# A hybrid decoder layer on one core: the triangular inverse from blocks of 16 and two levels of products, where blocks of 32 stood

## The chip, the cores and the metric

The kernel runs on one core of one Trainium2 chip. The metric is the device time of one execution in microseconds (us). The engines are TensorE (PE, with its weight loads as PEld), VectorE (DVE), ScalarE (ACT), GpSimd (POOL) and the queue engine SyncE (SP). Each takes its own instructions strictly in the order in which they were written, and waits at an instruction whose inputs aren't there.

## The reference, cut to what matters

One layer over 2048 tokens of width 1024. A projection feeds two branches: RWKV-7 time mixing (8 heads of 64) and forgetting attention (8 heads of 64). Both are gated, joined and projected out. The RWKV branch is a recurrence over the tokens:

```python
def step(S, inp):
    r_t, w_t, k_t, v_t, kk_t, b_t = inp
    sa = jnp.einsum('bhvk,bhk->bhv', S, kk_t)
    S = (S * w_t[:, :, None, :]
         - sa[..., None] * b_t[:, :, None, :]
         + v_t[..., None] * k_t[:, :, None, :])
    y = jnp.einsum('bhvk,bhk->bhv', S, r_t)
    return S, y
...
y_a = _rwkv7_scan(r_h, decay.reshape(hs), k_h, v_h, kk, kk * a_h)
y_b = _fox_attention(q_f, k_f, v_f, log_f).astype(x.dtype)
y = jnp.concatenate([y_a, y_b], axis=-1) * g_path
out = y @ w_out
```

## The kernel before, in words

**The stages.** Tokens go through in two halves of 1024. For each half there is an RWKV stage and an attention ("fox") stage; then comes the output projection. Beside them run the layer norm, the weight loads and the input projections: each projection tile is 24 products of 128x512 (`ps<-ht,wsp`), given out three at a time.

**RWKV by chunks.** The recurrence is done in chunks of 64 tokens. A block `n` (8 in each half) is one pair of heads and 512 tokens, that is 8 chunks for each of two heads: 16 triangular systems of 64x64, I + A with A strictly lower triangular, stored as `am`. For each block `rwkv_elem` makes the decays and normalised keys (DVE, ACT, POOL), `rwkv_scores` the score matrices (products 64x128, masked by DVE with `maskmm`), `rwkv_solve` the inverses of the triangular systems into `qt`, and `rwkv_batch` the outputs and the state, two chunks at a time, with the state updates one after the other. `rwkv_post` normalises the outputs. The blocks go in pairs: `elems` starts block n once block n-2 is done, so the solve of an even block runs beside `rwkv_elem` of the next one, and the solve of an odd block beside the batches of the even one.

**The solve before** (lines 1266 to 1337). The 64x64 systems are cut in blocks of 32. Four ACT copies put all 32 diagonal blocks (four on the partitions, eight along the free axis) in order, a DVE transpose replicates them, and then 31 pairs of tensor_tensors on DVE eliminate one column after the other (lines 1298 to 1304), each step needing the one before. Four transposes write the inverses of the diagonal blocks into `qt`, two more prepare `nt`, and two groups of sixteen 32x32 products on PE, each followed by two ACT copies, make the lower left block.

**What sets the order.** A planner written in Python (`Driver`) runs all streams as generators against a model of the engines: `cost` (lines 167 to 193) says how long an instruction takes, and of the streams that can go on the one with the earliest time, then the lowest priority number, writes its next instructions. Projections have priority 5, the solve 0. Which projection products stand between two products of the solve is thus fixed when the kernel is built. The planner's price of an ACT copy is `(94 if sb else 51) + 0.834 * n` ns (line 181), of a DVE tensor_tensor `69 + 1.04 * n` (line 188); no engine's work lengthens another's in it. All calls pass through one helper, so that nearly every row of the profile names line 134; the rows are told apart by tiles: `rw_s` is the arena of an RWKV stage, `ht,wsp` a projection, `wsp<-wst,wsp` the split of a weight on POOL, `fx_s`, `fx_p` and `fx_v` attention, `ps` PSUM.

Of the kernel before, what the change touches and what calls it, by code (L numbers as in the profile page):

```python
# [288 lines left out]
def hymba_kernel(ctx: ExitStack, tc, x, c, emb_ln_g, emb_ln_b, w_ada, b_ada, w_in, rwkv_mix, w0,  # L289
                 w_up, a0, a_up, k_k, k_a, r_k, gn_g, gn_b, fox_bf, w_out, ln_g, ln_b, out):  # L290
    nc = tc.nc
    drv = Driver()
# [25 lines left out]
    LA = ()  # L318
    LG = (2, 2, 4, 4)
    EF = 4  # L320
    NT = 1
    WD = 3
    XL = 5
    XN = 2
# [10 lines left out]
    pb = Banks(drv, ps, range(8))  # L335
# [11 lines left out]
    def mm(o, l, r, start=True, stop=True):  # L347
        pe.matmul(o, l, r, start=start, stop=stop, skip_group_check=True)
# [181 lines left out]
    def start_consts():  # L530
# [3 lines left out]
        yield  # L534
        ts(ident, jf, 0.0, None, OP.is_equal)
        yield
        dve.memset(nhalf, -0.5)
        pool.memset(mneg, 0.0)
        ts(mneg[:, 384:512], jf, 0.0, -1e30, OP.is_gt, OP.mult)
# [726 lines left out]
    def rwkv_solve(n, u, qt):  # L1266


        while not rw.solver:
            yield 0  # L1270
        qq, mt = rw.solver.pop()
        while not rw.nt:
            yield 0
        nt_ = rw.nt.pop()
        am = u.am.ap.rearrange("p (c a s) -> p c a s", c=2, s=64)
        nt = nt_.ap.rearrange("p (k a x) -> p k a x", k=2, x=32)
        lo = lambda ci: slice(64 * ci, 64 * ci + 32)
        hi = lambda ci: slice(64 * ci + 32, 64 * ci + 64)
        ad = qq.ap[:, 0:256].rearrange("p (s a) -> p s a", a=8)
        for ci in range(2):  # L1280
            for j in range(2):
                r0 = 64 * ci + 32 * j
                act.activation(ad[r0:r0 + 32].rearrange("p s a -> p a s"), am[r0:r0 + 32, ci, :, 32 * j:32 * j + 32],
                               AF.Copy)
        for ci in range(2):
# [3 lines left out]
        u.amuse -= 1  # L1289
        if not u.amuse:  # L1290
            u.am.free()
        M = mt.ap.rearrange("p (s r) -> p s r", r=32)
        dve.transpose(M, ad[:, :, :, None].to_broadcast([128, 32, 8, 4]))
        yield
        Q = qq.ap[:, 0:256].rearrange("p (a b) -> p a b", b=32)
        act.activation(Q, qinit, AF.Copy)
        yield
        for j in range(31, 0, -1):
            i0, k = j // 4, 8 - j // 4
            t = qq.ap[:, 256:256 + k * j].rearrange("p (a b) -> p a b", b=j)  # L1300
            tt(t, Q[:, i0:8, j:j + 1].to_broadcast([128, k, j]), M[:, j:j + 1, 0:j].to_broadcast([128, k, j]), OP.mult)
            yield
            tt(Q[:, i0:8, 0:j], Q[:, i0:8, 0:j], t, OP.subtract)
            yield
        while n >= 2 and n - 2 not in u.done:
            yield 0
        yield
        qv = qt.ap.rearrange("p (a b) -> p a b", b=128)
        for ci in range(2):
            for j in range(2):  # L1310
                r0 = 64 * ci + 32 * j
                dve.transpose(qv[r0:r0 + 32, :, r0:r0 + 32].rearrange("p a (i y) -> p i a y", y=4), Q[r0:r0 + 32])
        rw.solver.append((qq, mt))
        yield
        for ci in range(2):
            dve.transpose(nt[lo(ci), 1], qv[lo(ci), :, lo(ci)])
        yield
        b = yield from pb.get()
        for a in range(8):
            for ci in range(2):  # L1320
                mm(b.ap[hi(ci), a * 32:a * 32 + 32], nt[lo(ci), 0, a, :], nt[lo(ci), 1, a, :])
        yield
        for ci in range(2):
            act.activation(fl(nt[hi(ci), 1]), b.ap[hi(ci), 0:256], AF.Copy)
        b.free()
        yield
        b = yield from pb.get()
        for a in range(8):
            for ci in range(2):
                mm(b.ap[lo(ci), a * 32:a * 32 + 32], nt[hi(ci), 1, a, :], qv[hi(ci), a, hi(ci)])  # L1330
        yield
        for ci in range(2):
            act.activation(qv[lo(ci), :, hi(ci)], b.ap[lo(ci), 0:256].rearrange("p (a x) -> p a x", x=32), AF.Copy,
                           scale=-1.0)
        b.free()
        rw.nt.append(nt_)
        yield

    def rwkv_batch(p, n, c0, bufs, u, qt, yb, dl, st):
# [127 lines left out]
    def rwkv_stream(half):  # L1467

        phase_open(f"rw{half}", F32)
        sl = phase["slots"]  # L1470
        rw.solver = [(sl.now(1), sl.now(2))]
        rw.nt = [sl.now(1) for _ in range(NT)]
        rw.z = deque()
        rw.split = [0]
        rw.qt = [sl.now(2) for _ in range(2)]
# [560 lines left out]
```

## Time and profile before

| | |
|---|---|
| median of 3 runs | 1923.14 us (1916.16 to 1923.27) |
| the profiled execution | 1914.13 us, span 1912.4 us |
| busy in the span: PE | 1786.4 us (93%) |
| DVE | 1474.0 us (77%) |
| ACT | 781.2 us (41%) |
| POOL | 777.3 us (41%) |
| mean granted clock of PE | 0.973 of full speed |

The span runs from the first to the last instruction; the execution's time adds what lies around it. Busy time counts an instruction from start to end, also where it is held up while running. PE's products are pipelined, so that the mean of one is longer than its share of the time. The two RWKV stages lie at about 100 to 620 and 860 to 1350 us.

### The profile page before, as it was taken

Reading aid. Unit: us, or ns where it says so; the run is one execution under the profiler, and the core shown is the slowest. Engines: PE = TensorE matmul, PEld = TensorE weight load, DVE = VectorE, ACT = ScalarE, POOL = GpSimd, SP = SyncE. Lnnn points to the kernel's source line nnn. Section 1 sums busy time; section 2 is a strip of 40 time slices with the busy share of each in tenths; the row PEclk is TensorE's granted clock in tenths of the full one; section 3 lists DMA queues with packets and bytes.
Section 4 is the critical chain, followed back from the end, with each engine's and each line's share of the span. In section 5 each row is a group of like instructions: output and inputs, shape, how many; then the busy total and the mean of one; then the engine's idle time right before and its main releaser. Section 6 shows DMA issues by size and latency. Waiting matters only on the chain.

```text
span 1912.4 us, 30878 instructions
## 1 busy us (share of the span) xinstructions
PE 1786.4 (93%) x11049; PEld 1278.3 (67%) x11049; DVE 1474.0 (77%) x3606; ACT 781.2 (41%) x1507; POOL 777.3 (41%) x773
## 2 busy tenths in 40 slices
PE   8989989989899999999998999989999999999997
PEld 6667667767677755676676776667755564547876
DVE  5887897778874688568778887777367787877998
ACT  3464444533543266454453443533224444451000
POOL 1322341332423176633233331333216647675653
PEclk9999999989999999999999998989989998999999
DMA  9231110122113764332111121112365234213442
GB/s 282 66 120 63 51 54 23 39 66 62 44 51 94 238 197 127 99 108 71 45 44 43 47 65 34 52 47 89 122 209 165 93 114 136 79 61 107 141 138 105
DMA packets 172114, 181.31 MB, mean 95 GB/s; under 512 B 12181, under 2 KB 116198, under 8 KB 171961
## 3 DMA queue, kind: packets, MB, share of 16 engines
q1 hardware_dynamic: 171960, 179.33, 30.4%
q8 instruction: 88, 1.44, 0.3%
q14 instruction: 66, 0.53, 0.1%
HBM read 132.10 MB, written 47.13 MB: 94 GB/s over the span
## 4 chain that ended last, share of the span: by engine, by line
PE 45%; DVE 37%; ACT 6%; issue 4%; DMA 4%; POOL 3%; SPq 2%; POOLq 0%; DVEq 0%; ACTq 0%
PE ps L134 45%; DVE rw_s L134 19%; DVE arena L134 8%; ACT rw_s L134 4%; DVE small L134 4%; DVE end_s L134 3%; SPq L134 2%; DVE state L134 2%; DVE fx_p L134 1%; DMA wst<-in_w_in_dram 1%; DVE ht L134 1%; POOL wsp L134 1%; ACT arena L134 1%; POOL small L134 1%; DMA arena<-vscr 1%
## 5 line engine op out<-in xcount | busy, mean ns | idle before, releaser
L134 PE MATMUL ps<-ht,wsp 128*128 128x512 f32 x3840 | 981.3, 403 | 4.2 <-POOL wsp L134 3.5
L134 PEld LDWEIGHTS ps<-ht,wsp 128*128 128x128 f32 x3840 | 707.5, 191 | 161.0 <-issue 10.0
L134 DVE TENSOR_TENSOR rw_s<-rw_s 128x60 f32<-128x60 f32 (+24 forms) x1056 | 335.6, 321 | 51.2 <-ACT rw_s L134 24.0
L134 POOL TENSOR_TENSOR wsp<-wst,wsp 128x1024 fp32r<-128x1024 f32 x79 | 195.2, 2471 | 312.5 <-ACT wsp L134 267.8
L134 ACT ACTIVATE rw_s<-ps 64x256 f32<-64x256 f32 (+2 forms) x448 | 181.7, 418 | 264.4 <-PE ps L134 134.0
L134 PE MATMUL ps<-fx_s 67*128 67x512 f32 (+5 forms) x960 | 257.5, 390 | 4.4 <-ACT mrow L134 2.3
L134 PE MATMUL ps<-rw_s 32*32 32x32 f32 (+3 forms) x2816 | 208.2, 253 | 54.6 <-DVE rw_s L134 48.0
L134 PEld LDWEIGHTS ps<-fx_s 67*128 67x128 f32 (+1 forms) x960 | 164.2, 192 | 129.8 <-issue 70.3
L134 PEld LDWEIGHTS ps<-rw_s 32*32 32x32 f32 (+3 forms) x2816 | 179.4, 161 | 95.5 <-issue 55.9
L134 ACT ACTIVATE fx_p<-ps 128x512 f32<-128x512 f32 (+3 forms) x336 | 160.6, 521 | 182.7 <-PE ps L134 165.1
L134 POOL TENSOR_TENSOR fx_p<-fx_p 128x512 f32<-128x512 f32 (+2 forms) x160 | 188.9, 1186 | 109.1 <-PE ps L134 104.4
L134 POOL TENSOR_TENSOR small<-small,nhalf 128x8 f32<-128x8 f32 (+1 forms) x48 | 70.9, 1480 | 258.1 <-DVE small L134 174.8
L134 PE MATMUL ps<-fx_p,fx_v 128*64 128x512 f32 (+3 forms) x640 | 159.6, 559 | 1.6 <-POOL fx_p L134 1.6
L134 DVE TENSOR_TENSOR fx_p<-fx_p 128x512 f32<-128x512 f32 (+1 forms) x128 | 111.5, 871 | 64.1 <-POOL fx_p L134 62.2
L134 DVE TENSOR_REDUCE small<-ps 128x1 f32<-128x512 f32 (+1 forms) x208 | 133.8, 684 | 32.9 <-PE ps L134 32.1
L134 ACT ACTIVATE arena<-ps 128x512 f32<-128x512 f32 (+3 forms) x130 | 75.0, 579 | 174.1 <-PE ps L134 169.8
L134 ACT ACTIVATE wsp<-wst 128x1024 fp32r<-128x1024 f32 x80 | 84.2, 1053 | 143.0 <-PE ps L134 69.6
L134 POOL TENSOR_TENSOR rw_s<-rw_s,arena 128x512 f32<-128x512 f32 x64 | 82.5, 1294 | 136.9 <-ACT arena L134 89.6
L134 DVE TENSOR_TENSOR arena<-ps,arena 128x512 fp32r<-128x512 f32 (+4 forms) x108 | 73.2, 678 | 43.7 <-ACT arena L134 40.7
L134 DVE STREAM_TRANSPOSE rw_s<-rw_s 32x256 f32<-32x256 f32 (+1 forms) x112 | 61.6, 550 | 55.3 <-ACT rw_s L134 52.8
L134 ACT ACTIVATE rw_s<-rw_s 32x256 f32<-32x256 f32 (+1 forms) x144 | 83.4, 601 | 19.2 <-DVE rw_s L134 17.7
L134 DVE TENSOR_SCALAR state<-ps,dl 64x64 f32<-64x64 f32 x256 | 72.3, 282 | 19.3 <-PE ps L134 13.0
(147 smaller groups left out, 1885.2 us busy)
## 6 DMA issues: line engine op xcount, KB each, us to landing
wst<-in_w_in_dram SPq DMA_DIRECT2D x66, 512.0 KB
fx_s<-kscr SPq DMA_DIRECT2D x144, 128.0 KB
fx_s<-qscr SPq DMA_DIRECT2D x96, 128.0 KB
ada_t<-in_w_ada_dram SPq DMA_DIRECT2D x16, 512.0 KB
rw_l<-lowscr SPq DMA_DIRECT2D x32, 256.0 KB
kscr<-arena SPq DMA_DIRECT2D x32, 256.0 KB
qscr<-arena SPq DMA_DIRECT2D x32, 256.0 KB
arena<-in_x_dram SPq DMA_DIRECT2D x16, 512.0 KB
```

Source lines behind the costliest of these rows:

```text
L134: return fn(*args, **kw)
```

## The change

The diagonal blocks that are solved step by step are of 16, not 32. DVE does 15 pairs of tensor_tensors on both 16-blocks of each 32-block at once (two blocks in one access pattern). Two transposes then give the 16-block inverses in both orientations. A first group of 32 products, 16 wide and on the four diagonal corners of the array, with one scalar_tensor_tensor on DVE (which uses the new constant `u32`), and a second group of 48 products make the inverses of the 32-blocks; four ACT copies write these to `qt` and two keep what the last level needs in `x`. Two more groups of 16 products with two ACT copies each make the lower left 32-block, as before, with A read from `am` in place. The slot of `nt` goes, one slot `xu` comes. `u32` is made by three small operations at the start.

```diff
-        for ci in range(2):
-            with drv.side():
-                act.activation(nt[lo(ci), 0], am[lo(ci), ci, :, 32:64], AF.Copy)
...
-        for j in range(31, 0, -1):
-            i0, k = j // 4, 8 - j // 4
-            t = qq.ap[:, 256:256 + k * j].rearrange("p (a b) -> p a b", b=j)
-            tt(t, Q[:, i0:8, j:j + 1].to_broadcast([128, k, j]), M[:, j:j + 1, 0:j].to_broadcast([128, k, j]), OP.mult)
+        for j in range(15, 0, -1):
+            k = 4 - j // 4
+            o = (4 - k) * 32
+            t = qq.ap[:, 256:256 + 2 * k * j].rearrange("p (b i c) -> p b i c", b=2, c=j)
+            tt(t, blocks(qq.ap, 144, o + j, [32, k], [0, j]), blocks(mt.ap, 528, j * 32, [0, k], [1, j]), OP.mult)
             yield
-            tt(Q[:, i0:8, 0:j], Q[:, i0:8, 0:j], t, OP.subtract)
+            q = blocks(qq.ap, 144, o, [32, k], [1, j])
+            tt(q, q, t, OP.subtract)
             yield
...
-                dve.transpose(qv[r0:r0 + 32, :, r0:r0 + 32].rearrange("p a (i y) -> p i a y", y=4), Q[r0:r0 + 32])
...
-            dve.transpose(nt[lo(ci), 1], qv[lo(ci), :, lo(ci)])
...
-                mm(b.ap[hi(ci), a * 32:a * 32 + 32], nt[lo(ci), 0, a, :], nt[lo(ci), 1, a, :])
...
+        dve.transpose(dt.rearrange("p a (i y) -> p i a y", y=4), Q)
+        yield
+        dve.transpose(d, dt)
+        yield
+        b = yield from pb.get()
+        for a in range(8):
+            for r, ci, c in quads:
+                mm(b.ap[r, a * 16:a * 16 + 16], am[r, ci, a, c], d[r, a, 0:16])
+        yield
+        dve.scalar_tensor_tensor(tu[:, :, 0:16], b.ap[:, 0:128].rearrange("p (a x) -> p a x", x=16), u32[:, 32:33],
+                                 u32[:, None, 0:16].to_broadcast([128, 8, 16]), op0=OP.mult, op1=OP.add)
+        b.free()
...
+        b = yield from pb.get()
+        for a in range(8):
+            for r, ci, c in quads[0:2]:
+                mm(b.ap[r, 256 + a * 32:288 + a * 32], dt[r, a, :], tu[r, a, :])
+        for a in range(8):
+            for r, ci, c in quads[2:4] + quads[0:2]:
+                mm(b.ap[r, a * 32:a * 32 + 32], tu[r, a, :], dt[r, a, :])
+        yield
+        qv = qt.ap.rearrange("p (a b) -> p a b", b=128)
+        for r, ci, c in quads[0:2]:
+            act.activation(fl(x[r]), b.ap[r, 256:512], AF.Copy)
+        with drv.side():
+            for r, ci, c in quads[2:4] + quads[0:2]:
+                act.activation(qv[r, :, r], v8(b.ap[r, 0:256]), AF.Copy)
+            b.free()
+        yield
+        b = yield from pb.get()
+        for a in range(8):
+            for ci in range(2):
+                mm(b.ap[hi(ci), a * 32:a * 32 + 32], am[lo(ci), ci, a, 32:64], x[lo(ci), a, :])
```

**What stands where now.** The planner writes a new order from this. First PE, in the first half, from the last row-wise broadcast of block 3's `rwkv_elem` (`ident,rw_s`) to its second scores (`rw_s 128x128 x8`); before:

```order
L134 MATMUL ps<-ident,rw_s 128x128 x4
L134 MATMUL ps<-ht,wsp 128x512 x27
L134 MATMUL ps<-rw_s 128x128 x8
L134 MATMUL ps<-ht,wsp 128x512 x18
L134 MATMUL ps<-rw_s 128x128 x8
```

and now, at the same place:

```order
L134 MATMUL ps<-ident,rw_s 128x128 x4
L134 MATMUL ps<-ht,wsp 128x512 x24
L134 MATMUL ps<-rw_s 32x16 x32
L134 MATMUL ps<-ht,wsp 128x512 x3
L134 MATMUL ps<-rw_s 32x32 x48
L134 MATMUL ps<-ht,wsp 128x512 x3
L134 MATMUL ps<-rw_s 128x128 x8
L134 MATMUL ps<-rw_l,bones 128x512 x2
L134 MATMUL ps<-rw_s 32x32 x16
L134 MATMUL ps<-ht,wsp 128x512 x3
L134 MATMUL ps<-rw_s 128x128 x8
```

Block 2's solve, which stood behind block 3's scores before, now has its first two groups ahead of them.

Second PE, at the solve of block 3, which runs beside the batches of block 2 (`state,rw_s` and `rw_s,state` are one state step); before:

```order
L134 MATMUL ps<-rw_s,bones 32x128 x4
L134 MATMUL ps<-ht,wsp 128x512 x3
L134 MATMUL ps<-rw_s 32x32 x16
L134 MATMUL ps<-ident,rw_s 128x128
L134 MATMUL ps<-ht,wsp 128x512 x6
L134 MATMUL ps<-rw_s 32x32 x16
L134 MATMUL ps<-ht,wsp 128x512 x6
```

and now:

```order
L134 MATMUL ps<-rw_s 128x128 x4
L134 MATMUL ps<-rw_s 32x16 x32
L134 MATMUL ps<-state,rw_s 64x64 x2
L134 MATMUL ps<-rw_s,state 64x64 x2
L134 MATMUL ps<-ht,wsp 128x512 x3
L134 MATMUL ps<-rw_s 32x32 x48
L134 MATMUL ps<-state,rw_s 64x64 x2
L134 MATMUL ps<-rw_s,state 64x64 x2
L134 MATMUL ps<-ht,wsp 128x512 x3
L134 MATMUL ps<-rw_s 32x32 x16
```

The odd block's solve now lies among the state steps of the block before it, where it stood after them.

Third DVE, at the end of block 2's solve, with the key normalisation of block 3 (`rw_s<-arena,params,ps`); now:

```order
L134 SCALAR_TENSOR_TENSOR rw_s<-arena,params,ps 128x512
L134 TENSOR_TENSOR rw_s<-rw_s 128x2x4
L134 TENSOR_TENSOR rw_s<-rw_s 128x512 x2
L134 STREAM_TRANSPOSE rw_s<-rw_s 128x8x8x4
L134 SCALAR_TENSOR_TENSOR arena<-ps,params,arena 128x511
L134 SCALAR_TENSOR_TENSOR arena<-car,params,arena 128x1
L134 COPY car<-ps 128x1
L134 TENSOR_TENSOR rw_s<-rw_s 128x4x2x64
L134 STREAM_TRANSPOSE rw_s<-rw_s 128x256
L134 TENSOR_TENSOR rw_s<-rw_s 128x4x128
L134 TENSOR_TENSOR rw_s<-rw_s,arena 128x512
L134 SCALAR_TENSOR_TENSOR rw_s<-ps,u_122 128x8x16
```

Before, solve steps stood between these operations and after them; now the last step is the second row. Over the whole order, 1212 and 1218 projection products stood between the first product of an RWKV stage and the first of the attention stage that follows it, in the first and the second half; now 1020 and 1026. The others stand in the attention stages.

## Rows read from the trace of the kernel before

**Rows 1.** The page's head: span; busy time, share, instructions of each engine.

```profile
span 1912.4 us, 30878 instructions
...
PE 1786.4 (93%) x11049; PEld 1278.3 (67%) x11049; DVE 1474.0 (77%) x3606; ACT 781.2 (41%) x1507; POOL 777.3 (41%) x773
```

**Rows 2.** Busy times by stretch; columns in the first row.

```profile
core 0: us, PE busy (x) PEld busy (x) DVE busy (x) ACT busy (x) POOL busy (x), PEclk, DMA share, GB/s
100.00:600.00 500.00, 457.57 (x3372) 350.63 (x3372) 400.28 (x1151) 226.17 (x440) 162.41 (x164) 0.96 0.19 59
...
660.00:860.00 200.00, 197.50 (x1076) 127.27 (x1074) 145.50 (x296) 111.55 (x223) 119.79 (x152) 1.00 0.46 144
870.00:1350.00 480.00, 439.79 (x3313) 336.72 (x3314) 379.24 (x1120) 212.32 (x420) 150.67 (x157) 0.96 0.18 53
...
1420.00:1745.00 325.00, 315.49 (x1441) 170.09 (x1440) 245.13 (x420) 143.01 (x293) 199.96 (x202) 0.98 0.33 104
```

**Rows 3.** Products by tile and shape: count | busy us, mean ns | idle before.

```profile
L134 PE MATMUL ps<-rw_s 128*128 128x128 f32 x768 | 107.3, 287 | 6.6 <-issue 3.6 <-ACT rw_s L134 3.0
...
L134 PE MATMUL ps<-ident,rw_s 128*128 128x128 f32 x352 | 66.8, 295 | 11.3 <-POOL rw_s L134 10.4 <-DVE rw_s L134 0.5 <-ACT rw_s L134 0.4
L134 PE MATMUL ps<-state,rw_s 128*64 128x64 f32 x512 | 54.9, 246 | 16.8 <-DVE state L134 6.6 <-DVE rw_s L134 5.3 <-ACT rw_s L134 3.3
...
L134 PE MATMUL ps<-rw_s 64*128 64x128 f32 x512 | 42.6, 312 | 28.1 <-DVE rw_s L134 28.1
...
L134 PE MATMUL ps<-rw_s 32*32 32x32 f32 x1024 | 27.8, 202 | 19.9 <-DVE rw_s L134 19.9
```

**Rows 4.** The page's group of DVE's tensor_tensors on rw_s, all shapes.

```profile
L134 DVE TENSOR_TENSOR rw_s<-rw_s 128x60 f32<-128x60 f32 (+24 forms) x1056 | 335.6, 321 | 51.2 <-ACT rw_s L134 24.0
```

**Rows 5.** DVE's groups by shape, columns as in rows 3.

```profile
L134 DVE TENSOR_TENSOR rw_s<-rw_s 128x512 f32<-128x512 f32 x64 | 47.4, 760 | 1.5
...
L134 DVE STREAM_TRANSPOSE rw_s<-rw_s 32x256 f32<-32x256 f32 x96 | 41.7, 434 | 2.4
...
L134 DVE TENSOR_TENSOR rw_s<-ps,rw_s 64x128 f32<-64x128 f32 x128 | 36.8, 287 | 20.6 <-PE ps L134 18.8
...
L134 DVE TENSOR_TENSOR rw_s<-rw_s 128x28 f32<-128x28 f32 x64 | 12.4, 195 | 1.7
```

**Rows 6.** Timeline around block 3's scores: start us, us, engine, operation [idle before].

```profile
262.75 2.39 POOL L134 TENSOR_TENSOR wsp<-wst,wsp 128x1024 fp32r<-128x1024 f32 x1
262.76 2.45 DVE L134 TENSOR_TENSOR rw_s<-rw_s 128x60 f32<-128x60 f32 x1
...
267.14 5.02 DVE L134 TENSOR_TENSOR rw_s<-rw_s 128x72 f32<-128x72 f32 x7
...
267.27 6.40 PE L134 MATMUL ps<-ht,wsp 128*128 128x512 f32 x27
...
267.63 3.91 POOL L134 TENSOR_TENSOR rw_s<-rw_s,arena 128x512 f32<-128x512 f32 x3 [0.82 <-ACT rw_s L134]
...
272.08 0.74 DVE L134 SCALAR_TENSOR_TENSOR rw_s<-arena,params,ps 128x512 f32<-128x512 f32 x1
...
277.50 2.08 PE L134 MATMUL ps<-rw_s 64*128 64x128 f32 x16 [3.84 <-DVE rw_s L134]
```

**Rows 7.** Timeline of PE at block 0's solve.

```profile
175.00 0.70 PE L134 MATMUL ps<-rw_s 32*32 32x32 f32 x32
175.63 1.66 PE L134 MATMUL ps<-ht,wsp 128*128 128x512 f32 x6
177.22 0.69 PE L134 MATMUL ps<-rw_s 32*32 32x32 f32 x32
```

**Rows 8.** Timeline of PE at a head sum.

```profile
323.75 0.46 PE L134 MATMUL ps<-rw_s,bones 128*32 128x128 f32 x8
324.14 0.97 PE L134 MATMUL ps<-ht,wsp 128*128 128x512 f32 x3
```

**Rows 9.** ACT's copies of a solve from PSUM and within SBUF.

```profile
L134 ACT ACTIVATE rw_s<-rw_s 32x256 f32<-32x256 f32 x96 | 56.9, 592 | 12.5 <-DVE rw_s L134 11.0
...
L134 ACT ACTIVATE rw_s<-ps 32x256 f32<-32x256 f32 x64 | 24.1, 376 | 54.1 <-PE ps L134 53.3
```

**Rows 10.** Timeline of PE in a long run of projection products.

```profile
1357.91 14.56 PE L134 MATMUL ps<-ht,wsp 128*128 128x512 f32 x63
```

More of the change, by code (lines that the diff above doesn't have):

```diff
@@ L320, in hymba_kernel @@
     EF = 4
-    NT = 1
     WD = 3
@@ L359, in hymba_kernel @@
     qinit = const.tile([128, 8, 32], mybir.dt.bfloat16, name="qinit")
+    u32 = const.tile([128, 33], F32, name="u32")
     nhalf = const.tile([128, 16], F32, name="nhalf")
@@ L536, in start_consts @@
         yield
+        dve.tensor_reduce(u32[:, 0:32], ident.rearrange("p (q c) -> p c q", c=32), AX.X, OP.add)
+        yield
+        dve.tensor_reduce(u32[:, 32:33], u32[:, 0:16], AX.X, OP.add)
+        yield
+        ts(u32[:, 32:33], u32[:, 32:33], -1.0, None, OP.add)
         dve.memset(nhalf, -0.5)
@@ L1270, in rwkv_solve @@
             yield 0
[L1271 to L1274, printed above, removed]
+        qq, mt, xu = rw.solver.pop()
         am = u.am.ap.rearrange("p (c a s) -> p c a s", c=2, s=64)
-        nt = nt_.ap.rearrange("p (k a x) -> p k a x", k=2, x=32)
         lo = lambda ci: slice(64 * ci, 64 * ci + 32)
         hi = lambda ci: slice(64 * ci + 32, 64 * ci + 64)
+        quads = [(slice(64 * ci + 32 * j, 64 * ci + 32 * j + 32), ci, slice(32 * j, 32 * j + 32))
+                 for j in range(2) for ci in range(2)]
+        v8 = lambda ap: ap.rearrange("p (a x) -> p a x", a=8)
         ad = qq.ap[:, 0:256].rearrange("p (s a) -> p s a", a=8)
-        for ci in range(2):
[L1281 to L1285, printed above, removed]
-            with drv.side():
-                act.activation(nt[lo(ci), 0], am[lo(ci), ci, :, 32:64], AF.Copy)
+        for r, ci, c in quads:
+            act.activation(ad[r].rearrange("p s a -> p a s"), am[r, ci, :, c], AF.Copy)
         yield
-        u.amuse -= 1
-        if not u.amuse:
-            u.am.free()
         M = mt.ap.rearrange("p (s r) -> p s r", r=32)
@@ L1297, in rwkv_solve, with blocks @@
         yield
-        for j in range(31, 0, -1):
-            i0, k = j // 4, 8 - j // 4
-            t = qq.ap[:, 256:256 + k * j].rearrange("p (a b) -> p a b", b=j)
-            tt(t, Q[:, i0:8, j:j + 1].to_broadcast([128, k, j]), M[:, j:j + 1, 0:j].to_broadcast([128, k, j]), OP.mult)
+        def blocks(t, step, off, *dims):
+            return bass.AP(tensor=t.tensor, offset=t.offset + off, ap=[list(t.ap)[0], [step, 2], *dims])
+        for j in range(15, 0, -1):
[3 more added lines that the diff above has]
+            tt(t, blocks(qq.ap, 144, o + j, [32, k], [0, j]), blocks(mt.ap, 528, j * 32, [0, k], [1, j]), OP.mult)
             yield
-            tt(Q[:, i0:8, 0:j], Q[:, i0:8, 0:j], t, OP.subtract)
+            q = blocks(qq.ap, 144, o, [32, k], [1, j])
+            tt(q, q, t, OP.subtract)
             yield
+        dt, d, x, tu = v8(mt.ap[:, 0:256]), v8(qq.ap[:, 256:512]), v8(mt.ap[:, 256:512]), v8(xu.ap[:, 0:256])
+        dve.transpose(dt.rearrange("p a (i y) -> p i a y", y=4), Q)
[4 more added lines that the diff above has]
+        for a in range(8):
+            for r, ci, c in quads:
+                mm(b.ap[r, a * 16:a * 16 + 16], am[r, ci, a, c], d[r, a, 0:16])
[3 more added lines that the diff above has]
+        b.free()
         while n >= 2 and n - 2 not in u.done:
@@ L1320, in rwkv_solve @@
             for ci in range(2):
-                mm(b.ap[hi(ci), a * 32:a * 32 + 32], nt[lo(ci), 0, a, :], nt[lo(ci), 1, a, :])
+                mm(b.ap[hi(ci), a * 32:a * 32 + 32], am[lo(ci), ci, a, 32:64], x[lo(ci), a, :])
         yield
         for ci in range(2):
-            act.activation(fl(nt[hi(ci), 1]), b.ap[hi(ci), 0:256], AF.Copy)
+            act.activation(fl(x[hi(ci)]), b.ap[hi(ci), 0:256], AF.Copy)
         b.free()
+        u.amuse -= 1
+        if not u.amuse:
+            u.am.free()
         yield
@@ L1470, in rwkv_stream @@
         sl = phase["slots"]
-        rw.solver = [(sl.now(1), sl.now(2))]
-        rw.nt = [sl.now(1) for _ in range(NT)]
+        rw.solver = [(sl.now(1), sl.now(2), sl.now(1))]
+        act.activation(rw.solver[0][2].ap[:, 0:256].rearrange("p (a x) -> p a x", x=32),
+                       u32[:, None, 0:32].to_broadcast([128, 8, 32]), AF.Copy)
         rw.z = deque()
```

14 lines of the change are left out of this document (4 added, 10 removed).

## The prediction

> **What bounds the kernel now.** I read the page's first lines, then the busy times by stage, then the products' groups, then one stall in order of time. [rows 1]: PE is busy for 1786.4 of 1912.4 us, DVE for 1474.0. A busy PE alone does not show which one limits, so the stages come next [rows 2]. The two RWKV stages (100 to 600 and 870 to 1350 us, the only ones that solve) keep PE busy for 457.6 of 500 and 439.8 of 480 us, DVE for 400.3 and 379.2. In the two attention stages PE is busy for 197.5 of 200 and 315.5 of 325 us. PE is never short of work as a whole: the projections, 512 columns wide, are laid into every hole of the RWKV stages, and what isn't done there is done beside attention. So a shorter chain of solve steps is no gain by itself. It moves projections to a later stage, where PE needs the same time for them. The total is PE's work, plus its waits, plus what a low clock costs.
>
> The waits of the RWKV stages are 42.4 and 40.2 us by rows 2 (stretch minus busy). [rows 3] says who waits: the score products (64x128) 28.1 us, the solve's 32x32 products 19.9, broadcasts 11.3, state products 16.8, the other 128x128 products 6.6; together 82.7 us. All of the first 48.0 are ended by DVE writing rw_s. The mean granted clock is 0.96 in both stages [rows 2], so about 4% of 980 us, 39 us, is lost to stretches at 1.2 GHz instead of 2.4 GHz. Waits and clock make 122 us: all that a faster solve can give back.
>
> [rows 6] shows how such a wait arises. From 267.27 PE has 27 projection products queued ahead of the scores, and they last until 273.7. DVE needs 5.02 us for seven solve steps from 267.14, while POOL's three tensor_tensors run from 267.63 for 3.91 us; one step just before took 2.45 us beside a POOL tensor_tensor of 2.39 us. A solve step alone takes about 0.2 us [rows 5]. The key normalisation on DVE, which the scores need, thus starts at 272.08, and the scores at 277.50, after 3.84 us of waiting. The planner's cost function (lines 167 to 193) knows nothing of this blocking.
>
> **DVE's part.** Of the 1056 tensor_tensors on rw_s (335.6 us) [rows 4] 64 are not the solve's (128x512, 47.4 us) [rows 5]. The other 992 are 16 solves of 62 steps: 288.2 us, 0.29 us each, blocking included. Now a solve has 30 steps of 8 to 44 elements (29 on average). The nearest row, 128x28, has 195 ns [rows 5]; I take 0.21, between it and the 0.29 of all steps: 480 steps, 101 us (94 to 139). Six transposes of 434 ns per solve [rows 5] become two of the same free width: 41.7 to 13.9 us. The new scalar_tensor_tensor from PSUM (128 elements) is like the 64x128 row of 287 ns [rows 5]: 4.6 us. DVE goes from 330 to about 120 us, 210 us less. None of it counts by itself: DVE is not the stages' bound, and only what PE waited for counts.
>
> **PE's part.** Two groups of sixteen 32x32 products per solve become four groups of 32 (16 wide), 48, 16 and 16. Each f32 product leaves two records. A group of 32 records takes 0.63 us from its first start to the next product's [rows 7], with two corners of the array in turn: some 0.5 us of records and 0.13 of tail. Between two such groups six projection products took 1.59 us (175.63 to 177.22), where a long run gives 0.231 each (14.56 us for 63) [rows 10], 1.39 for six: 0.1 us for each change of shape. The new first group and 32 products of the second use four corners in turn. No 32-wide row shows four at once. The nearest is the head sums with four column strips: 8 records of 128 columns in 0.39 us (323.75 to 324.14) [rows 8], 49 ns each, where full-array products of 128 columns have 140 ns (107.3 us for 768) [rows 3]. So I take four corners at the pace of two: first group 0.5, second 0.5 plus 0.5, and 0.4 us for the two extra groups' tails and changes of shape. That is 1.9 us per solve, **31 us** in 16. Bounds: 24 us if the 16-wide products take half as long and half of the tails is hidden; 48 us if four corners go no faster than two (1.0 and 1.5 us).
>
> Whether 16 columns save anything is a question on which a page has a rule: the Trainium skill, TensorEngine Tiling (Array Packing), Instruction Overhead, says that every matmul has about 60 cycles of overhead, so that a narrower one costs no less. By it the first group stays at 0.5 us; by width alone it would be 0.25, and the sum 4 us lower. No run here shows a 16-wide product yet.
>
> **The waits.** The order shows what PE now waits for. In an even block's solve (with the next block's scores to come) the first group stands, in the block shown, behind 24 projection products (5.5 us), and DVE must pass ahead of it: the normalisation (0.74) [rows 6], four 512-wide operations (0.7 each, near the 760 ns of rows 5), the token shift and two transposes; about 5.5 us, plus POOL's blocking of 1.3 (one of the three in rows 6) to 3.7 us. The wait, 1 to 4 us, moves from the scores to the solve; I take 2.4, and 0.4 for the second group, whose DVE operation stands behind two 512-wide ones. In an odd block's solve state steps stand between the groups, with three projection products (0.7 us) where twelve or six stood. I keep the present wait for the first group (1.2 us, half of 19.9 over 8 pairs), and add 0.5 for the second, behind eight PSUM additions, and 0.5 for the third and fourth: ACT's copies of 376 ns [rows 9] are priced at 264 by the planner (line 181), and four new ones of the diagonal stand ahead of the third group's. Per pair 5.0 us instead of 6.0 (48.0 in 8 pairs): **-8 us**. Bounds: +18 if nothing moves and 1.1 us of new waits comes to each solve; -30 if the score waits vanish and the others don't grow.
>
> The other 34.7 us of waits (broadcasts, states, ACT) stand behind a DVE queue that loses about a quarter of its work (105 of 400 us per stage): **-8 us** (0 to -17). The 39 us of clock follow the waits, a fifth less: **-8 us** (+6 to -20). ACT gets six more copies and two less of 592 ns per solve, and is at 226 of 500 us: nothing, unless it comes late as above. SP, POOL and DMA have the same work.
>
> **Sum.** +31 - 8 - 8 - 8 = +7 us on the profiled execution's 1914.1 us: 1921. The median of the runs, 1923.1, is 0.5% above that execution; on its scale 1930 us. What measurement can tell from no change is about 0.5%, 9.6 us.
>
> **Rivals.**
> 1. *The long chain of groups wins (slower).* Four groups in PE's order are four places at which projections can't pass. If all of the score wait moves to the first group and the new waits come on top, 31 + 18 us give 1963, on the median's scale 1972; with half of the 18 it is 1963 there. For: in the odd blocks three projection products cover a chain PE, ACT, PE of about 1 us. Against: DVE reaches the groups sooner. From 21 us of returned waits downward this case decides (31 less 10).
> 2. *DVE was late because of the solve (faster).* In [rows 6] solve steps hold DVE for 5.02 us between the broadcast and the normalisation, and more follow. If their absence ends half of the 48 us (-24), 14 of the other 34.7, and half of the clock's loss (-19), then 31 - 57 = -26: 1888, or 1897 on the median's scale. It decides when more than 41 of the 122 us come back. For: DVE has no slack when POOL blocks it. Against: POOL's tensor_tensors stay on the same path, and the order leaves fewer projections between two waits. A page bears on it: the Trainium skill, SBUF — State Buffer, Two separate sides, says that DVE operations with two SBUF inputs and GpSimd share a port pair that one holds for its whole instruction. The trace agrees (2.45 beside 2.39 us); half the steps would then also collide less often.
> 3. *DVE's steps don't get cheaper (slower).* If steps with two blocks in one access pattern take the 0.29 us of today or more, and half collide, DVE's saving halves, no wait comes back, half a microsecond of new ones per solve (8 us) comes to the 31, and 1914 + 39 gives 1953, on the median's scale 1962.
>
> **Chances.** Near-balance, within 10 us of 1923: 0.33. Rival 1: 0.29; rival 3: 0.09; rival 2: 0.29. So faster 0.29, same 0.33, slower 0.38. My own case by itself is 1913 to 1933. For 8 in 10 I cut a tenth from each side: down to rival 2's 1897 and a little below, 1895, and up to rival 3's 1962.
>
> **What would show it.** In the changed kernel's profile: 480 solve steps at 0.19 to 0.29 us, two transposes per solve; 32x16 and 32x32 records in groups of about 0.6, 1.1, 0.6 and 0.6 us; PE's waits for DVE before the scores falling from 28.1 us, those before the small products rising from 19.9; both RWKV stages about 40 us shorter and attention with more projections beside it. I am wrong if PE's small products cost much more or less than 31 us more, or if the RWKV stages' waits fall by a third or grow.

## The result, and the profile of the changed kernel

The changed kernel takes **1909.3 us** (median of 6 runs, 1903.1 to 1915.0), the kernel before 1921.5 in the same runs (1912.1 to 1923.8): a ratio of 0.9948, with a 95% interval of 0.9925 to 0.9971. It is faster by half a per cent. The forecast was 1930 us and no change or a slight loss. The profiled execution spans 1903.7 us at a granted clock of 0.968 (before: 1912.4 at 0.973).

The page's head of the changed kernel, beside [rows 1]:

```profile
span 1903.7 us, 35535 instructions
...
PE 1816.7 (95%) x13609; PEld 1307.2 (69%) x13609; DVE 1287.7 (68%) x3049; ACT 802.5 (42%) x1573; POOL 778.2 (41%) x773
```

PE is busy for 30.3 us more (the forecast had 31 for the products), and DVE for 186 less (forecast 210). PE's idle time, span less busy, falls from 126.0 to 87.0 us, by 39.0. Between the two profiled spans that makes 30.3 - 39.0 = -8.7 us. By stretches, beside [rows 2]:

```profile
100.00:600.00 500.00, 469.79 (x4658) 360.07 (x4657) 317.99 (x907) 237.14 (x477) 165.06 (x167) 0.95 0.19 56
...
870.00:1350.00 480.00, 459.46 (x4674) 353.93 (x4672) 313.27 (x909) 227.99 (x465) 157.80 (x163) 0.98 0.21 63
...
1420.00:1745.00 325.00, 319.55 (x1408) 186.68 (x1408) 220.97 (x359) 121.57 (x237) 178.39 (x163) 0.96 0.37 118
```

In these stretches PE waits for 30.2 and 20.5 us (42.4 and 40.2 before). The stages themselves, from their first product to the first of the attention stage behind them, last 488 and 468 us instead of 526 and 527. The products of the same stages, beside [rows 3] (count | busy us, mean ns | idle before, and what ended it):

```profile
L134 PE MATMUL ps<-rw_s 128*128 128x128 f32 x768 | 105.7, 283 | 5.0 <-ACT rw_s L134 4.1 <-DVE car L134 0.4
L134 PE MATMUL ps<-ident,rw_s 128*128 128x128 f32 x352 | 65.1, 288 | 8.8 <-POOL rw_s L134 7.0 <-ACT rw_s L134 1.3
L134 PE MATMUL ps<-state,rw_s 128*64 128x64 f32 x512 | 51.3, 249 | 8.9 <-ACT rw_s L134 4.6 <-DVE state L134 3.7
L134 PE MATMUL ps<-rw_s 32*32 32x32 f32 x2560 | 51.0, 209 | 3.4 <-issue 2.1 <-DVE rw_s L134 0.6 <-ACT rw_s L134 0.5
...
L134 PE MATMUL ps<-rw_s 64*128 64x128 f32 x512 | 42.2, 311 | 1.5 <-DVE rw_s L134 1.5
...
L134 PE MATMUL ps<-rw_s 32*32 32x16 f32 x1024 | 12.4, 185 | 24.1 <-DVE rw_s L134 24.1
```

The wait of the scores (64x128) went from 28.1 us to 1.5. That of the solve's products is 27.5 (19.9 before), 24.1 of it ahead of the first group (32x16) and only 3.4 ahead of the other three. Scores and solve together: 48.0 before, 29.0 now, 40 forecast. The other three groups of [rows 3] went from 34.7 to 22.7 (26.7 forecast).

DVE's groups by shape, beside [rows 5]:

```profile
L134 DVE TENSOR_TENSOR rw_s<-rw_s 128x512 f32<-128x512 f32 x64 | 50.7, 813 | 1.6
...
L134 DVE TENSOR_TENSOR rw_s<-rw_s 128x24 f32<-128x24 f32 x96 | 35.9, 374 | 2.7
...
L134 DVE STREAM_TRANSPOSE rw_s<-rw_s 128x256 f32<-128x256 f32 x32 | 14.2, 443 | 0.8
L134 DVE TENSOR_TENSOR rw_s<-rw_s 128x36 f32<-128x36 f32 x64 | 13.7, 214 | 1.4
```

A step that nothing holds up takes about 0.2 us (128x36: 214 ns); those of 24 elements have 374 ns in the mean, since some are held up by POOL. In the whole trace 22 of the 480 solve steps took more than 0.4 us, and each of them ended within 0.1 us of the end of a POOL operation that it overlapped; before, this befell 72 of 992. Beyond 0.2 us a step, that is some 23 us of DVE's time now and 80 before. The place of [rows 6] in the changed kernel (timeline, all engines):

```profile
270.09 2.97 DVE L134 TENSOR_TENSOR rw_s<-rw_s 128x24 f32<-128x24 f32 x7
...
271.10 1.29 POOL L134 TENSOR_TENSOR rw_s<-rw_s,arena 128x512 f32<-128x512 f32 x1 [0.46 <-ACT rw_s L134]
271.12 5.72 PE L134 MATMUL ps<-ht,wsp 128*128 128x512 f32 x24
...
274.51 2.85 POOL L134 TENSOR_TENSOR wsp<-wst,wsp 128x1024 fp32r<-128x1024 f32 x1 [2.12 <-ACT wsp L134]
...
278.58 0.73 PE L134 MATMUL ps<-rw_s 32*32 32x16 f32 x64 [1.74 <-DVE rw_s L134]
```

The solve is finished sooner, so 24 projection products cover nearly the whole of DVE's path to the first group; 1.74 us are left, and the scores find their operands ready.

### The profile page after: what moved, and what is told of

It reads as the page before. It is cut to its first block, busy times and chain, and to the rows that moved or that the text cites. A ratio compares the mean times of both kernels' runs of the same rounds, so it can differ in the third digit from the quotient of the medians.

```text
span 1903.7 us, 35535 instructions
## 1 busy us (share of the span) xinstructions
PE 1816.7 (95%) x13609; PEld 1307.2 (69%) x13609; DVE 1287.7 (68%) x3049; ACT 802.5 (42%) x1573; POOL 778.2 (41%) x773
## 3 DMA queue, kind: packets, MB, share of 16 engines
q1 hardware_dynamic: 171960, 179.33, 30.3%
## 5 line engine op out<-in xcount | busy, mean ns | idle before, releaser
L134 ACT ACTIVATE rw_s<-ps 64x256 f32<-64x256 f32 (+3 forms) x544 | 215.6, 408 | 212.6 <-PE ps L134 111.9
L134 PE MATMUL ps<-rw_s 32*32 32x32 f32 (+4 forms) x5376 | 238.7, 227 | 34.1 <-DVE rw_s L134 26.3
L134 PEld LDWEIGHTS ps<-rw_s 32*32 32x32 f32 (+3 forms) x5376 | 207.9, 140 | 86.6 <-DVE rw_s L134 32.9
L134 POOL TENSOR_TENSOR fx_p<-fx_p 128x512 f32<-128x512 f32 (+2 forms) x160 | 184.9, 1162 | 114.9 <-PE ps L134 111.2
L134 DVE TENSOR_TENSOR rw_s<-rw_s 128x24 f32<-128x24 f32 (+11 forms) x544 | 164.3, 306 | 23.3 <-ACT rw_s L134 9.5
L134 DVE TENSOR_TENSOR fx_p<-fx_p 128x512 f32<-128x512 f32 (+1 forms) x128 | 107.4, 839 | 72.3 <-POOL fx_p L134 70.6
L134 DVE TENSOR_TENSOR arena<-ps,arena 128x512 f32<-128x512 f32 (+4 forms) x108 | 72.8, 675 | 77.5 <-ACT arena L134 58.5
L134 POOL TENSOR_SCALAR rw_s<-rw_s 64x128 f32<-64x128 f32 x128 | 38.0, 296 | 114.0 <-PE ps L134 103.5
L134 ACT ACTIVATE rw_s<-rw_s 32x256 f32<-32x256 f32 (+2 forms) x112 | 69.8, 651 | 27.2 <-DVE rw_s L134 26.5
```

The source lines that it names most:

```text
L134: return fn(*args, **kw)
```

## The experiments

The planner charges an operation when it adds the cost to its model. An operation that is charged but not issued (a ghost), or issued but not charged, leaves the order as it was: in the traces of runs 1, 2, 3, 5 and 9 the projection products stand in the same places among the others as in the kernel whose order they keep. The ratio is to runs of before on the same chip. "Idle" is the profiled span less PE's busy time; "clock" is one less the granted clock, times the span: half of the time that PE stood at 1.2 GHz. The two overlap, since PE also idles in slow stretches. Constant 69 is the base cost, in ns, of a DVE operation in the planner's cost function (line 188); another constant gives the same work in another order. In the expectations theory A is that the gain comes from DVE's shorter queue; its rivals are that it comes from the new order (B), that the new products cost little (C), or that the luck of an order decides (D).

| run | median us | ratio to before, 95% | idle | clock |
|---|---|---|---|---|
| before (69) | 1921.5 | 1 | 126.0 | 51.6 |
| changed (69) | 1909.3 | 0.9925 to 0.9971 | 87.0 | 60.9 |
| 1 before, 32 of 62 steps of a solve not issued | 1884.1 | 0.9782 to 0.9838 | 106.1 | 52.8 |
| 2 changed, two groups' products doubled | 1979.8 | 1.0293 to 1.0372 | 113.9 | 80.8 |
| 3 changed, 30 steps added | 2017.0 | 1.0489 to 1.0549 | 153.7 | 112.7 |
| 4 before, 71 | 1960.4 | 1.0188 to 1.0243 | 147.1 | 86.0 |
| 5 both terms of the change in before's order | 1891.1 | 0.9844 to 0.9904 | 86.1 | 47.2 |
| 6 changed, 71 | 1905.6 | 0.9904 to 0.9955 | 93.1 | 49.4 |
| 7 before, 67 | 1952.6 | 1.0150 to 1.0216 | 143.0 | 89.8 |
| 8 changed, 67 | 1904.5 | 0.9914 to 0.9963 | 89.1 | 60.9 |
| 9 the same in the order of run 4 | 1917.2 | 0.9981 to 1.0032 | 98.8 | 69.0 |
| 10 before, 70 | 1937.5 | 1.0068 to 1.0128 | 142.0 | 79.4 |
| 11 changed, 70 | 1898.3 | 0.9852 to 0.9928 | 85.9 | 54.9 |
| 12 changed, one operation off POOL | 1896.7 | 0.9866 to 0.9933 | 93.5 | 39.8 |
| 13, 14 the same at 70, 71 | 1899.1, 1904.0 | 0.9892 to 0.9949, 0.9908 to 0.9959 | 94.8, 96.0 | 49.6, 36.1 |
| 15 before, POOL's blocking planned | 1933.5 | 1.0044 to 1.0102 | 135.3 | 99.0 |
| 16 **changed, POOL's blocking planned** | **1838.3** | 0.9553 to 0.9630 | 70.8 | 16.5 |
| 17 as 16, at 71 | 1855.6 | 0.9653 to 0.9708 | 75.9 | 24.1 |
| 18 as 15, at 71 | 1905.5 | 0.9927 to 0.9970 | 117.7 | 81.9 |

**Run 1: DVE's relief alone.** The planner still charges all steps, so every engine's order is that of before.

```diff
-            tt(Q[:, i0:8, 0:j], Q[:, i0:8, 0:j], t, OP.subtract)
...
+            for ops, op in zip(two, (OP.mult, OP.subtract)):
+                if j > 15:
+                    drv.time(dve, "tensor_tensor", ops, {})
+                else:
+                    tt(*ops, op)
```

> The kernel before with its order of instructions kept exactly as it is, but with the solve steps of j = 31 to 16 (32 of the 62 steps of each solve) not issued; that part of the elimination is left out. PE's work is that of before; DVE loses 512 steps, about 150 us at 0.29 us each. Theory A (DVE was late because of the solve: its shorter queue alone took PE's waits away): PE's idle time falls by about 30 us or more, and the time by as much, to 1880 to 1893 us, 1.5 to 2.2% below before. Rival B (the waits went because the new order puts other things between them, not because DVE has less to do): at most 10 us come back, 1911 us or more.

34 us came back (28 between the profiled spans: 20 of idle time, where theory A had 30 or more, and 8.5 of PE's busy time). The products' rows:

```profile
L134 PE MATMUL ps<-state,rw_s 128*64 128x64 f32 x512 | 47.4, 246 | 8.0 <-DVE state L134 3.9 <-ACT rw_s L134 3.4
...
L134 PE MATMUL ps<-rw_s 64*128 64x128 f32 x512 | 37.2, 284 | 11.3 <-DVE rw_s L134 11.3
...
L134 PE MATMUL ps<-rw_s 32*32 32x32 f32 x1024 | 29.5, 208 | 25.9 <-DVE rw_s L134 25.9
```

The scores wait 16.8 us less, the states 8.8 less; the solve's products 6.0 more. Theory A holds, with a smaller share of idle time than it had: a shorter DVE queue gives PE waits back without a new order.

**Runs 2 and 3: each load put back into the changed kernel.**

```diff
+        for a in range(8):
+            for r, ci, c in quads:
+                again(b.ap[r, a * 16:a * 16 + 16], am[r, ci, a, c], d[r, a, 0:16])
...
+            for _ in range(2):
+                dve.eng.tensor_tensor(t, blocks(qq.ap, 144, o + j, [32, k], [0, j]),
+                                      blocks(mt.ap, 528, j * 32, [0, k], [1, j]), op=OP.mult)
```

The first lines are run 2's, where `again` issues a product without charging it (the second group is repeated in the same way); the last are run 3's.

> The changed kernel, its order kept, with the products of the first and the second group of each solve issued twice (the same results), some 160 more records per solve. By the measured 0.66 us and 1.16 us of these groups, less their tails, that is 1.6 us of PE per solve, 26 us in 16. Theory A (PE is the bound, every microsecond of added product is paid): 26 us above the changed kernel, 1.3 to 1.4%, so 1935 us, about 0.8% above before. Rival C (the new small products lie in time in which PE would have waited, so that they cost little, which is why the change gained): at most 8 us above the changed kernel, still not above before.

> The changed kernel, its order kept, with each of the 15 multiplies of a solve issued three times (the same results): 30 more DVE steps per solve, 480 in all, about 114 us at 0.237 us each, some three fifths of what the change took from DVE. Theory A (DVE's shorter queue took the waits away): PE waits again, 15 to 25 us more, the time 0.8 to 1.3% above the changed kernel, back at or above before. Rival B (the new order did it): at most 6 us more (0.3%).

Both cost more than expected. Run 2 took 70 us instead of 26. The groups grew from 0.66 to 1.19 us, and from 1.16 to about 2.4 (first product to the next), 28 us in all. The rest is in these rows of it, in the word "issue":

```profile
L134 PE MATMUL ps<-rw_s 32*32 32x32 f32 x2560 | 53.8, 212 | 8.0 <-issue 7.9
...
L350 PE MATMUL ps<-rw_s 32*32 32x32 f32 x1536 | 26.8, 212 | 19.2 <-issue 19.2
```

These are 27 us in which PE stood at the groups of small products, in bursts of up to 192 records, and waited for nothing that the profile shows; in the changed kernel it is 2.1 us. The clock lost another 20, in part in the same stretches. So the added products are paid in full (rival C falls), but the size is not one of products alone. In run 3, 93 us more of busy DVE cost 108 us: 67 of idle and 52 of clock, which overlap.

```profile
L134 PE MATMUL ps<-ident,rw_s 128*128 128x128 f32 x352 | 68.3, 299 | 41.8 <-POOL rw_s L134 40.0 <-ACT rw_s L134 1.3
L134 PE MATMUL ps<-state,rw_s 128*64 128x64 f32 x512 | 58.2, 265 | 27.8 <-ACT rw_s L134 17.7 <-DVE state L134 8.7 <-DVE rw_s L134 0.5
...
L134 PE MATMUL ps<-rw_s 32*32 32x16 f32 x1024 | 13.2, 189 | 37.8 <-DVE rw_s L134 36.0 <-DVE small L134 1.8
```

The names of POOL and ACT stand there because they come last, but only DVE was changed: a late DVE is seen as waits for the engines that it feeds. In a fixed order, DVE work that the planner hadn't charged cost its whole length here, and work taken out gave back three tenths (34 of 117 us in run 1).

**Runs 4, 6 to 8, 10, 11: other orders of the same work.**

```diff
-            return 69 + 1.04 * n + ptr
+            return 71 + 1.04 * n + ptr
```

The other runs have 67 or 70.

> The kernel before with one constant of the planner's cost of a DVE operation changed from 69 to 71 ns. No work changes; only the planned order of the instructions does, in many places. It tells how much of half a per cent can be luck of the order. Theory A (the gain is DVE's): within 0.3% of before. Rival D (any new order moves this kernel by half a per cent either way, so that the gain of the change needs no cause): 0.4% or more from before, in either direction.

> The changed kernel with the planner's constant 69 changed to 71, which moved the kernel before by 2.2%. Rival D (the order's luck decides): another time than the changed kernel's 1909, by 0.5% or more in either direction; before with 71 had 1960, so if the change is worth something by itself, this one is below 1960. Theory A (DVE's relief makes the kernel robust against a bad order, since less waits for DVE): the spread is smaller than before's 2.2%, 1900 to 1930, and the change would gain 1.5 to 3% at this constant.

> The kernel before with the planner's constant 67 for 69: a third order of the same work. If the order of before is a lucky one (rival D), above 1918 us by 0.5 to 2.5%; if the spread is symmetric about it, as likely below.

> The changed kernel with the planner's constant 67 for 69. Theory A: below the kernel before at the same constant by more than the 0.5% that the change gained at 69, as DVE has slack; 1900 to 1930. Rival D: no relation between the two, with a difference of either sign.

> The kernel before with the planner's constant 70 for 69: a fourth order. At 67 and 71 it had 1953 and 1960 us, at 69 1918. If 69 is a lucky order: 1935 to 1965 us. If the time changes smoothly about 69: 1925 to 1945.

> The changed kernel with the planner's constant 70 for 69. At 67, 69 and 71 it had 1904, 1909 and 1906 us. Theory A (with DVE's slack the order matters little): 1898 to 1915. Rival D: outside of that.

This changed the question. 2 ns in a cost make the kernel before 2.2% slower, so theory A's 0.3% for run 4 was wrong and rival D right. At 67, 69, 70 and 71 it has ratios of 1.018, 1, 1.010 and 1.022: 69 is the best of the four. The changed kernel has 0.994, 0.995, 0.989 and 0.993, all three new ones in the ranges of theory A. By constant the change gains 2.4, 0.5, 2.1 and 2.9%; the means are 1.0124 and 0.9927. Over four orders the change is worth **about 2%**, and half a per cent only beside the best order of before. About half of what separates an unlucky order from 69 is clock: between the profiled spans of run 4 and before lie 43 us, 21 of idle time and 22 of busy time of the same products, where the clock lost 34 more (a part of it while PE idled).

**Runs 5 and 9: both terms, no new order.** 48 of 62 steps off, products tripled.

```diff
+                if j > 7:
+                    drv.time(dve, "tensor_tensor", ops, {})
...
+        for _ in range(2):
+            for a in range(8):
+                for ci in range(2):
+                    again(b.ap[hi(ci), a * 32:a * 32 + 32], nt[lo(ci), 0, a, :], nt[lo(ci), 1, a, :])
```

The second group is repeated in the same way.

> The kernel before with its order kept, and both terms of the change put into it without a new order: solve steps j = 31 to 8 (48 of 62 per solve) are not issued (that part of the elimination is left out), which takes DVE to about the changed kernel's busy time, and each of the two groups of small products is issued three times, four groups of about half a microsecond more per solve, about 2 us of PE as in the change. By the first ghost (32 steps off, 1884 us) and 16 further steps, 1870 to 1884 without the products. Theory A (the gain is the sum of the two terms: DVE's relief of 30 to 45 us less PE's 30 us): 1900 to 1915 us, 0.3 to 1.1% below before, near the changed kernel. Rival B (the new order is what gains): no better than before, 1918 us or more. Rival D (the new order loses, and hides a larger gain of the two terms): under 1895 us.

> As the run that put both terms into the order of before (48 of 62 steps of each solve not issued, that part of the elimination left out; the two groups of small products issued three times), but in the order that constant 71 gives, which by itself had 1960 us. Theory A (that order is slow because DVE is late in it; with DVE's work gone the two orders come together): 1885 to 1905 us, 55 to 75 us back from 1960 although 32 us of products are added. Rival D (the order itself costs the 42 us, whoever is late): 1920 to 1940, the 27 us that the same edit gave in before's order.

Run 5 is 1.3% below before with DVE's busy time (1286.1 us) and idle time of the changed kernel; its products:

```profile
L351 PE MATMUL ps<-rw_s 32*32 32x32 f32 x2048 | 44.2, 202 | 0.0
...
L134 PE MATMUL ps<-rw_s 64*128 64x128 f32 x512 | 37.2, 284 | 5.6 <-DVE rw_s L134 5.6
...
L134 PE MATMUL ps<-rw_s 32*32 32x32 f32 x1024 | 27.7, 202 | 18.7 <-DVE rw_s L134 18.7
```

It came out below theory A's 1900 to 1915, on rival D's side: the two terms alone gain 27 us here. By the ratios the changed kernel is 14 us slower (0.9948 beside 0.9874), as much as its clock loses more (60.9 us beside 47.2). That its new order does this is likely but not shown, since it also has more ACT copies (802.5 us of ACT beside 781.0) and other product shapes. Run 9 gave 43 us in the order of run 4, between the two expectations and nearer to rival D's: it stays 26 us above run 5, 22 of it clock, where the orders by themselves lie 42 apart. So both hold in part: a light DVE closes some of the distance between two orders, and some of it is the order's.

**Runs 12 to 14: one operation moved from POOL to DVE.**

```diff
-        tt(t.ap, t.ap, K.ap, OP.mult, pool)
+        tt(t.ap, t.ap, K.ap, OP.mult)
```

> The changed kernel with one tensor_tensor per block of the key path (the product of the token shift with K) on DVE instead of POOL; the planner makes its order anew. DVE has slack now, and POOL's tensor_tensors hold DVE's operations up for their whole length. Theory A (DVE's slack can take work from POOL): POOL about 20 us less, DVE about 11 us more, PE's waits before broadcasts (8.8 us, ended by POOL) and the small products (24 us) fall by 5 to 10 us: 1895 to 1905. Rival: the path is as long on DVE; within 0.3% of 1909, as other orders of the changed kernel are.

> The changed kernel with the product of the token shift with K on DVE instead of POOL, at constant 70 (1898 us without the move). At 69 the move gave 1897 beside 1909, but PE waited no less (82 us beside 76) and the clock was higher. If the move itself is worth something: 0.3% or more below 1898. If it was only another order: 1898 give or take 0.4%.

> The same move at constant 71 (1906 us without it). If the move itself is worth something: 1900 us or less. If it was only another order: 1898 to 1912, on either side of 1906.

By the ratios it is 0.5% less at 69 (in theory A's range), 0.3% more at 70 and the same at 71, and PE's idle time is higher each time. The move is worth nothing that can be told from another order.

**Runs 15 to 18: a planner that knows of the blocking.** In its clock (`time`, behind `e.began = max(t, e.free)`):

```diff
+        two = e.name == "dve" and "tensor_tensor" in op and sum(
+            i.space != "PSUM" and i.free_size() > 1 for i in ins) > 1
+        if two and self.pool.began <= e.began < self.pool.free:
+            e.began = self.pool.free
```

A DVE tensor_tensor on two SBUF inputs that would begin while POOL is at work is planned for POOL's end.

> The kernel before, planned with one more rule: a DVE tensor_tensor on two SBUF inputs that would begin while a POOL operation runs begins at that operation's end. The work is that of before, only the order is new. If the unlucky orders of before come from a planner that is blind to this blocking: at or below before's 1918 us, 1895 to 1918, with less PE waiting than 115 us. If an order's luck has other causes: like the other orders of before, 1935 to 1960.

> The changed kernel, planned with the same rule. If the blocking is what its order misses: 1880 to 1897 us, below the 1898 to 1909 of its four orders, with the small products' wait (24 us in the changed kernel) falling. If not: 1897 to 1912.

> The changed kernel planned with POOL's blocking, at constant 71. If the rule is what gives 1838 us: 1830 to 1860. If that was one lucky order: 1885 to 1910, as the changed kernel's other orders.

> The kernel before planned with POOL's blocking, at constant 71 (1960 us without the rule, 1934 with it at 69). If the rule serves the old solve too, and the attention stage's half clock in the run at 69 was an order's bad luck: 1870 to 1910 us. If DVE with the long solve has no slack to plan with: 1925 to 1960.

With the changed solve this gives **1838.3 us**, 4.1% below before and 3.6% below the changed kernel, for the same work in another order. It is far below the 1880 to 1897 expected; at 71 it is 1855.6, within 1830 to 1860. Run 16's products:

```profile
L134 PE MATMUL ps<-ident,rw_s 128*128 128x128 f32 x352 | 63.2, 282 | 3.5 <-POOL rw_s L134 2.8 <-ACT rw_s L134 0.5
L134 PE MATMUL ps<-state,rw_s 128*64 128x64 f32 x512 | 48.0, 246 | 5.1 <-ACT rw_s L134 2.4 <-DVE state L134 2.4
...
L134 PE MATMUL ps<-rw_s 32*32 32x32 f32 x2560 | 44.5, 193 | 5.6 <-ACT rw_s L134 2.9 <-DVE rw_s L134 2.3 <-issue 0.2
...
L134 PE MATMUL ps<-rw_s 32*32 32x16 f32 x1024 | 11.6, 180 | 4.7 <-DVE rw_s L134 4.6
```

The first group waits 4.7 us instead of 24.1. At the place shown above, PE now has 42 projection products ahead of it instead of 24 (timeline of run 16):

```profile
263.19 9.79 PE L134 MATMUL ps<-ht,wsp 128*128 128x512 f32 x42
275.07 0.73 PE L134 MATMUL ps<-rw_s 32*32 32x16 f32 x64 [2.10 <-DVE rw_s L134]
```

At this one place the wait is no shorter (2.10 us beside 1.74); the other fifteen solves make up the 2.6 that are left. The rule doesn't free DVE: 27 solve steps are held up for more than 0.4 us (22 without it), and DVE is busy for 1306.7 us (1287.7). It makes the plan expect DVE later, and PE gets more to do in the meantime: the RWKV stages now hold 1119 and 1125 projection products (1020 and 1026 without the rule). No run prices DVE higher without regard to POOL, so it isn't shown that the gain needs this rule rather than any plan with a later DVE.

Idle falls by 16 us, but the clock's loss by 44, and its stages run at 1.00, 0.99 and 0.99 (windows of run 16):

```profile
100.00:600.00 500.00, 483.24 (x4829) 374.19 (x4827) 337.64 (x938) 241.70 (x486) 170.47 (x169) 1.00 0.23 69
...
870.00:1350.00 480.00, 466.41 (x4497) 358.14 (x4495) 310.61 (x865) 226.32 (x461) 162.90 (x167) 0.99 0.25 76
1420.00:1745.00 325.00, 314.02 (x1442) 201.61 (x1441) 261.41 (x408) 114.96 (x222) 196.30 (x168) 0.99 0.34 109
```

The old solve gains by the rule at 71 (1960 to 1906, as expected if the rule serves it) and loses 0.7% at 69 (1933.5, just under the 1935 to 1960 of the other expectation). Windows of run 15, whose profiled execution (1943.8 us) is the slowest of ten, say where that went:

```profile
100.00:600.00 500.00, 476.90 (x3382) 368.70 (x3382) 397.26 (x1080) 223.14 (x426) 169.34 (x157) 0.98 0.24 73
...
870.00:1350.00 480.00, 456.38 (x3232) 348.99 (x3231) 369.36 (x1032) 212.86 (x407) 170.99 (x159) 0.98 0.27 84
1420.00:1745.00 325.00, 291.15 (x1342) 164.00 (x1342) 235.68 (x474) 116.68 (x246) 154.14 (x165) 0.87 0.30 92
...
886.00:1492.00 606.00, 547.59 (x3769) 416.48 (x3768) 476.98 (x1275) 239.49 (x463) 211.45 (x189) 0.94 0.27 84
1450.00:1492.00 42.00, 15.46 (x113) 11.18 (x114) 28.89 (x65) 6.23 (x15) 11.57 (x8) 0.66 0.32 105
```

In the first two stretches PE waits for 23.1 and 23.6 us, 36 less than before, but in the third for 33.9 at 0.87. That loss isn't attention's: in this order the second RWKV stage lasts from 886 to 1492 us, 606 us where it had 527. The plan laid 1572 and 1425 projection products into the two RWKV stages (1212 and 1218 before), and from 1454 to 1785 us none was left. In the last state steps and the change to attention nothing covered PE's waits; in the 42 us to 1492 it was busy for 15.5, and the longest wait was 12.9 us for one DMA (timeline of run 15):

```profile
1475.43 1.11 PE L134 MATMUL ps<-ident,rw_s 128*128 128x128 f32 x4 [6.07 <-POOL rw_s L134]
1489.48 1.11 PE L134 MATMUL ps<-ident,arena 128*128 128x128 f32 x4 [12.93 <-DMA arena<-vscr]
```

By whole stages, the RWKV stages wait 34.3 and 58.4 us (42.9 and 43.1 before). With the light solve the same rule asks for fewer projections, and they last into attention.

## Why the prediction was wrong

- *PE's products, +31 us: right.* Busy time rose by 30.3. At 2.4 GHz a solve's groups take 0.66, 1.16, 0.62 and 0.62 us from first product to the next, some 2.0 us more than before with the changes of shape (1.9 forecast). Four corners run at the pace of two, as taken, and 16 columns save nothing: 0.66 less a tail of 0.13 is the forecast's 0.5. By the rule of the Trainium skill (TensorEngine Tiling (Array Packing), Instruction Overhead), a narrower product costs no less; the trace agrees: the 64 records of 16 columns take about 0.5 us, and so do the 64 of 32 columns on four corners in the second group. Busy time holds the clock's share too. The solve's own rows go from 27.8 to 63.4 us, and to 56.1 in run 16, where the clock was nearly full: some 28 to 36 us more.
- *DVE's steps: nearly right.* 480 steps at 0.24 us (0.21 forecast); rival 3 falls, since under a third as many steps are held up.
- *Scores and solve, -8 us: the failed step.* It moved the score wait to the first group rightly (2.3 us in the mean of the even blocks, 2.4 forecast), but it added waits that didn't come. In the odd blocks the first group waits 0.7 us (1.2 forecast), the second 0.02 (0.5), the third and fourth under 0.1 (0.5). The measured term is -19. By the prediction's own sign it was wrong if the RWKV stages' waits fell by a third; in the stretches of [rows 2] they fell from 82.6 to 50.7 us.
- *The other waits, -8 us: too small.* States, broadcasts and 128x128 products gave 12 us, and 8 more came from waits outside the products of [rows 3], which the sum left out. All waits together: -39 instead of -16, and these 23 us decide the direction. Run 1 shows the reason: DVE's queue alone, in before's own order, gives the scores 16.8 us and the state steps 8.8.
- *The clock, -8 us: not there.* Between the two profiled executions it cost 9 more, of which the executions' own scatter is a good part (the medians of the clock are 0.970 before and 0.969 now). In the RWKV stages, where the forecast wanted a fifth less, it is 36 us before and 37 now. It doesn't follow the waits in proportion: at 0.968 the changed kernel idles for 87 us, at 0.973 the kernel before for 126.

Rival 2 had the mechanism: DVE was late because of the solve. Its price, 41 of 122 us to decide, was not reached at 69 (39 of waits back, 9 of clock lost), and its 1897 us is about what other orders gave (1898 to 1906). What none of the cases had is the order of before as a quantity with a spread of 2%, at whose best end the comparison was made: the half per cent is the change less that advantage. Whether 69 came about by choice or by luck no run shows, and the trace of one order cannot show the spread.

The blocking in [rows 6] was told rightly, and its weight in the plan was missed. By the Trainium skill (SBUF — State Buffer, Two separate sides) DVE operations on two SBUF inputs and GpSimd take turns on one port pair; the trace agrees in the 22 held steps above, each of which ended with a POOL operation. What runs 16 and 17 show is the worth of a plan that reckons with it: by the ratios 3.6 and 2.5% below the changed kernel at the same constant.

## What to carry to other kernels

Where a planner sets the order, vary one of its costs by a few per cent before and after a change, and compare the spreads: here one comparison gave 0.5%, and four gave about 2%. To split a change, keep the order and leave out or repeat single terms without charging them. And a plan should reckon with what holds an engine up: the blocking rule gained 3.6 and 2.5% in two orders with the light solve; with the heavy one it lost 0.7% and gained 2.6%. A rule that lays more filling work into one stage can leave none for its end, so look at where the filling runs out.

## What was not expected of the hardware

- Around bursts of 128 and 192 records of small products (32x32 tiles) PE stood still for 0.5 to 3.6 us at a time and waited for nothing that the profile shows ("issue", 27 us in run 2); with 64 and 96 records in the changed kernel it is 2.1 us in all. No run here tells the cause.
- The clock can outweigh the waits: run 16 has 16 us less idle time than the changed kernel and 44 us less of clock loss. In run 15 one stretch of 82 us, from the uncovered end of the second RWKV stage into attention, ran at half clock (1.2 GHz) throughout (windows of it):

```profile
1463.00:1545.00 82.00, 53.30 (x150) 31.55 (x150) 53.93 (x122) 12.51 (x26) 14.13 (x15) 0.50 0.28 83
1550.00:1745.00 195.00, 194.84 (x906) 100.03 (x906) 144.60 (x280) 92.90 (x194) 119.49 (x132) 1.00 0.32 99
```

PE was busy for 53 of the 82 us; in the 195 from 1550 on, busy for 194.8, it had 2.4 GHz.
